# Where 11 modulation sums are worked off, and two later steps for a pair of transposes

## The chip, the cores and the metric

The kernel runs on one core of one Trainium2 chip. The metric is the device time of one launch in microseconds (us): 2756.03 us is the median of three runs before the change (2755.0 to 2768.02). One more execution was profiled; its rows are quoted below.

## What is computed

Two transformer blocks over 256 tokens of width 2048, all in fp32. The part that matters here is the first block, and a piece of the second.

```python
mod = silu(c) @ w_ada + b_ada              # c: one row of 2048, w_ada: 2048 x 12288
sh1, sc1, gt1, sh2, sc2, gt2 = split(mod, 6)
h = modulate(rms_norm(x, g_mix), sh1, sc1)
z = h @ w_in                               # heads q, k, v of two kinds, an indexer, two gates
o_sb = stick_breaking_attention(...)       # 8 heads
o_ds = indexer_sparse_attention(...)       # indexer scores, best 64 keys a query, 8 heads
merged = sigmoid(gate_sb) * (o_sb @ w_o_sb) + sigmoid(gate_ds) * (o_ds @ w_o_dsa)
x = x + gt1 * (merged @ w_out)
h = modulate(rms_norm(x, g_ffn), sh2, sc2) # then a gated FFN with sc2, sh2, gt2
```

The second block has its own projections, 8 heads of a sparse attention (compressed, selected and window branches: `nsa_head`), 8 heads of a forgetting attention (`fox_head`), an output projection and an FFN.

## The kernel before

**Weights.** Every fp32 weight tile (128 x 1024, 512 KB, two k-slices of a 512-column group) is loaded by SyncE into one of 6 buffers `raw` (L127), split by ScalarE into a high part `wh` (L296, 4 buffers) and by VectorE into the rest `wl` (L303, 4 buffers), and then multiplied: in a group with `pair` two matmuls a slice and 128-column strip (L344, L345; L341, L342 for the first), otherwise three (L347 to L349). A strip is accumulated in one of four PSUM tiles `pg`; when its last slice is in, its evacuation (ScalarE and VectorE, L452/L453 for gates, L1050 and L1062 for the two merges) frees it for the next group. Weight tiles are split three tiles ahead of their matmuls (`AHEAD`, L368, `split_to`, L389).

**Modulation sums.** The products with `w_ada` don't run on TensorE. `w_ada` is held transposed; a half row block (128 x 1024, again 512 KB in a `raw` buffer) is multiplied by the broadcast row `cb` and summed by one VectorE instruction (L311). Two such sums give 128 values of `mod`; 192 sums are in the kernel. They stand in the same list of items as the weight tiles, and both are loaded, split and summed in the order of that list, so where a sum is put into the list decides whose neighbour it is on SyncE and on VectorE.

**The list.** `add_group` (L985) appends a group's weight tiles, and after each tile it adds `rate` to a credit; when the credit reaches 1 it appends one sum. In the stretch of the change the groups follow each other so (each with 8 weight tiles, the projections' with 4):

- `ggs[0]` to `ggs[3]` (L1033): the first gate's 16 strips, four groups. Beside them run the last heads of the stick-breaking attention, then `bias_table` (L713, which writes a table `tabs` of 1.5 MB to DRAM), the scoring of `indexer` (L738), and its eight rounds of picking keys.
- four groups of `w_o_sb` (L1054), the first projection of heads, which beside the running sums of `indexer` on GpSimd (L795) merge into the gates.
- `ggs[4]` to `ggs[7]` (L1056): the second gate, with the 8 sparse heads of block one.
- four groups of `w_o_dsa` (L1086), the second projection of heads; each strip is merged by VectorE (L1062) and GpSimd (L1063) and split for the next product by ScalarE (L477) and GpSimd (L479).
- what is left: `while ada_rest and ada_rest[0][2]` (L1087) appends the rest of a begun block of eight sums, the others go to `ada_late` (L1089), which four groups of `w_out` take up at 0.75 a tile, from the fifth tile on.

A program walk through this list gives, for the sums after each group's tiles: 4, 6, 7, 7 in `ggs[0]` to `ggs[3]`; 7 in `w_o_sb`; 8, 7, 7, 7 in `ggs[4]` to `ggs[7]`; 7 in `w_o_dsa`, 1 left, and 16 in `w_out`.

**Steps.** The attention parts are Python generators. `spent` (L323) advances all of them by one step for every 1.27 us of nominal matmul time (`TICK`), so that their instructions stand at fixed places between the matmuls. `yield from wait(3)` passes three steps. `seq` (L690) starts one `nsa_head` every 7 steps. A head computes two score tiles, two softmax tiles (`t`, tag `t2`, two buffers), scales them by rows, passes `W` = 3 steps (L1538), transposes both (L1539, L1540, six matmuls of L846), copies them and multiplies by the values. `fox_chain` (L1636) begins when the last `nsa_head` is done, one head every 5 steps; the second half of the output projection first drains it (L1696): the rest of its steps is issued with no weight matmuls between.

Of the kernel before, what the change touches and what calls it, by code (L numbers as in the profile page):

```python
# [26 lines left out]
W = 3  # L27
# [6 lines left out]
RL = (0.75, 0.6)  # L34
MORE = 12
SPARE = 5
RA = (0.6, 0.7, 0.9, 0.9, 0.45)
GAPS = (5, 7)

LAND = 45  # L40
# [81 lines left out]
def kernel(ctx: ExitStack, tc: tile.TileContext, t):  # L122
# [97 lines left out]
    def wait(n):  # L220
        for _ in range(n):
            yield

    def drain(gens):
        while any(g in active for g in gens):
            tick()
# [13 lines left out]
    def w_items(g):  # L240
        return [("w", [g], k, n) for k, n in pieces(g.nk, g.width)]
# [200 lines left out]
    def copy(out_, in_, scale=None):  # L442
        if alt():
            nc.scalar.activation(out=out_, in_=in_, func=AF.Copy, scale=1.0 if scale is None else scale)
        elif scale is None:
            nc.vector.tensor_copy(out=out_, in_=in_)
        else:
            nc.vector.tensor_scalar(out=out_, in0=in_, scalar1=float(scale), scalar2=None, op0=OP.mult)
# [217 lines left out]
    def av_out(a, vs, o_pair, h, extra=None):  # L666

        O = psm()
        if not isinstance(a, list):
            a = [a]  # L670
        for half in range(2):
            o = O[:, 128 * half:128 * half + 128]
            mms = []
            if extra is not None:
                mms.append((extra[0], extra[1][:, 128 * half:128 * half + 128]))
            for p, (v, c) in zip(a, vs):
                if half == 0:
                    mms.append((v[:, 0, c:c + 128], p[:, 0:128]))
                else:
                    mms.append((v[:, 0, c:c + 128], p[:, 128:256]))  # L680
                    mms.append((v[:, 1, c:c + 128], p[:, 256:384]))
            for n, (l, r) in enumerate(mms):
                nc.tensor.matmul(o, l, r, start=(n == 0), stop=(n == len(mms) - 1))  # L683
        yield
        hi, lo = o_pair(h)
        nc.scalar.activation(out=hi, in_=O[:, :T], func=AF.Copy)
        yield
        nc.vector.tensor_sub(out=lo, in0=O[:, :T], in1=hi.bitcast(F32))
# [123 lines left out]
    def scores(q, k):  # L812

        S = psm()
        nc.tensor.matmul(S[:, 0:128], q[:, 0:128], k[:, 0:128], start=True, stop=True)
        nc.tensor.matmul(S[:, 128:384], q[:, 128:256], k, start=True, stop=True)  # L816
        return S

    def softmax(S, add, pool, shift=None):

        p = pool.tile([128, 384], F32, name="t2", tag="t2")
        st = pool.tile([128, 6], F32, name="st", tag="st", bufs=4)
        for b, (o, n) in enumerate(BLK):
            nc.vector.tensor_tensor_reduce(out=p[:, o:o + n], in0=S[:, o:o + n], in1=add[:, o:o + n], scale=1.0,  # L824
                                           scalar=-3.4e38, op0=OP.add, op1=OP.max, accum_out=st[:, b:b + 1])
        if shift is None:
            nc.vector.tensor_scalar(out=st[:, 2:4], in0=st[:, 0:2], scalar1=-1.0, scalar2=None, op0=OP.mult)
        else:
            nc.vector.tensor_add(out=st[:, 0:2], in0=st[:, 0:2], in1=shift)
            nc.vector.tensor_sub(out=st[:, 2:4], in0=shift, in1=st[:, 0:2])  # L830
        yield
        for b, (o, n) in enumerate(BLK):
            lut(out=p[:, o:o + n], in_=p[:, o:o + n], func=AF.Exp, bias=st[:, 2 + b:3 + b],
                accum_out=st[:, 4 + b:5 + b])
        yield
        return p, st

    def scale_rows(p, r):
        for b, (o, n) in enumerate(BLK):
            nc.vector.tensor_scalar(out=p[:, o:o + n], in0=p[:, o:o + n], scalar1=r[:, b:b + 1], scalar2=None,  # L840
                                    op0=OP.mult)

    def transpose_p(p):
        PT = psm()
        for j in range(3):
            nc.tensor.transpose(PT[:, 128 * j:128 * j + 128], p[:, 128 * j:128 * j + 128], C["ident"])  # L846
        return PT
# [131 lines left out]
    ada_rest = extra + ada_at((2, 3, 8, 9, 10, 11, 4, 5, 6))  # L979
# [5 lines left out]
    def add_group(g, fill=None, rate=0.0, skip=0):  # L985
        for n, it in enumerate(w_items(g)):
            items.append(it)
            if n < skip:
                continue
            credit[0] += rate * it[3] * it[1][0].width / RAW if fill else 0.0  # L990
            while fill and credit[0] >= 1.0:
                items.append(fill.pop(0))
                credit[0] -= 1.0
# [36 lines left out]
    for u, g in enumerate(ggs[:4]):  # L1030
        if u == 1:
            g.pre = lambda: drain([gens["sb"]])
        add_group(g, ada_rest, RA[min(u, 2)])  # L1033

    def o_act(which):
        def act(k):
            return (*bufs["o_" + which](k), bufs["o_" + which].both(k))
        return act

    def sig(which, u):  # L1040
        def go():
            if u % 2 == 0:
                g = gates[which, u // 2]
                lut(out=g, in_=g, func=AF.Sigmoid)
        return go

    def merge1(u):
        def evac(f, ps):
            g = gates[0, u // 2][:, 4 * (u % 2) + f, :]
            nc.vector.tensor_mul(out=g, in0=ps[:, :T], in1=g)  # L1050
        return evac

    for u in range(4):
        add_group(Group("f", [(512, t["w_o_sb"], 512 * u, idr)], 8, o_act("sb"), merge1(u), pre=sig(0, u)), ada_rest, RA[4])  # L1054
    for g in ggs[4:]:
        add_group(g, ada_rest, RA[3])  # L1056

    def merge2(u):
        def evac(f, ps):
            k = 4 * u + f  # L1060
            g = gates[1, u // 2][:, 4 * (u % 2) + f, :]
            nc.vector.tensor_mul(out=g, in0=ps[:, :T], in1=g)  # L1062
            nc.gpsimd.tensor_tensor(out=g, in0=g, in1=gates[0, u // 2][:, 4 * (u % 2) + f, :], op=OP.add)  # L1063
            if k == 0:
                acts["m"] = Pair()
            pend(hilo_gen(*acts["m"](k), g))
        return evac
# [16 lines left out]
    for u in range(4):  # L1084
        add_group(Group("f", [(512, t["w_o_dsa"], 512 * u, idr)], 8, o_act("ds"), merge2(u),
                        pre=dsa_pre if u == 0 else sig(1, u)), ada_rest, RA[4])  # L1086
    while ada_rest and ada_rest[0][2]:  # L1087
# [436 lines left out]
    def nsa_head(h):  # L1524
        g, qh = h // 4, R["qn"][:, h, :]
        sd = R["t"].tile([128, 384], F32, name="t1", tag="t1")
        nc.scalar.activation(out=sd, in_=C["dist"], func=AF.Copy, scale=2.0 ** -(h + 1))
        yield
        S1 = scores(qh, R["kv"][:, 4 + g, :])
        yield  # L1530
        S2 = scores(qh, R["kv"][:, 6 + g, :])
        p1, st1 = yield from softmax(S1, sd, R["t"])
        p2, st2 = yield from softmax(S2, sd, R["t"])
        for i, (p, st) in enumerate(((p1, st1), (p2, st2))):
            nc.vector.reciprocal(out=st[:, 0:2], in_=st[:, 4:6])
            nc.vector.tensor_mul(out=st[:, 0:2], in0=st[:, 0:2], in1=R["gat"][:, 1 + i, h, :])
            scale_rows(p, st[:, 0:2])
        yield from wait(W)  # L1538
        PT1 = transpose_p(p1)  # L1539
        PT2 = transpose_p(p2)  # L1540
        yield
        pT = []
        for PT in (PT1, PT2):
            x = R["t"].tile([128, 384], F32, name="t3", tag="t3", bufs=3)
            copy(x, PT[:, :384])
            pT.append(x)
        yield from wait(W)
        j = h // 2
        vc = R["vcT"][32 * j:32 * j + 32, 128 * (h % 2):128 * (h % 2) + 128]
        yield from av_out(pT, [(R["vsw"], 128 * g), (R["vsw"], 256 + 128 * g)], oN(), h,  # L1550
                          extra=(vc, R["pcT"][32 * j:32 * j + 32, :]))
# [3 lines left out]
    def nsa_chain():  # L1555
        waits = gens["kn"] + gens["qn0"] + gens["qn1"] + [gens["cmp"]]
        while any(g in active for g in waits):
            yield
        yield from cmp_branch()
        yield  # L1560
        yield from seq([nsa_head(h) for h in range(8)], 7)
# [191 lines left out]
```

## Time and profile before

| | us |
|---|---|
| median of three runs | 2756.03 |
| the profiled execution, its time | 2759.37 |
| its span (first to last instruction) | 2757.6 |
| TensorE busy | 2666.0 (97%) |
| VectorE busy | 1982.8 (72%) |
| ScalarE, GpSimd busy | 1364.7, 542.1 |
| granted TensorE clock over the span | 0.991 |

The busy share is an average over stages. The rows below cut the stretch of the change at the first matmul of each group.

### The profile page before, as it was taken

To read this page: it belongs to the slowest core of one execution; us is meant where nothing else is said; L and a number is where in the kernel's file an instruction comes from. 1 tells how busy PE (TensorE), PEld (TensorE's weight loads), DVE (VectorE), ACT (ScalarE), POOL (GpSimd) and SP (SyncE) were. 2 spreads that over 40 slices of the span, in tenths; PEclk is the share of its full clock that TensorE was granted. 3 is DMA by queue.
4 is the path that set the end of the run, shared out by engine and by line. 5 is a ranking of instruction groups with operands and counts; after the bars stand their busy time and mean duration, and the time that the engine had idled before them with its cause. 6 is when DMAs were issued, how large, how long until landed. Compare 5 with 4: busy or idle time off the path is not lost. (4 is left out here: it accounts for less than half of the span.)

```text
span 2757.6 us, 42269 instructions
## 1 busy us (share of the span) xinstructions
PE 2666.0 (97%) x15956; PEld 2336.8 (85%) x15956; DVE 1982.8 (72%) x2882; ACT 1364.7 (49%) x2067; POOL 542.1 (20%) x506
## 2 busy tenths in 40 slices
PE   6899999899998999999999999999999999999999
PEld 5788897798977888888888878888888888888888
DVE  7998986998887876556666756677876665566655
ACT  4554563354446555434555535555555544345443
POOL 1654420210612010000011301102222210012210
PEclk8999999999998999999999999999999999999999
DMA  8888867889986876666666675544566666666664
GB/s 324 264 267 262 260 215 201 277 278 334 311 276 202 299 251 186 194 188 189 189 183 198 188 221 154 161 125 150 175 184 185 195 192 192 191 190 189 189 199 143
DMA packets 302044, 591.16 MB, mean 214 GB/s; under 512 B 20996, under 2 KB 60780, under 8 KB 301710
## 3 DMA queue, kind: packets, MB, share of 16 engines
q1 hardware_dynamic: 298214, 583.61, 66.1%
q10 hardware_dynamic: 3626, 4.85, 0.8%
q8 instruction: 125, 2.05, 0.3%
q14 instruction: 79, 0.65, 0.1%
HBM read 582.54 MB, written 5.78 MB: 213 GB/s over the span
## 5 line engine op out<-in xcount | busy, mean ns | idle before, releaser
L345 PE MATMUL pg<-ring,wh 128*128 128x512 f32 x5408 | 1903.5, 393 | 3.8 <-DVE ring L1165 3.8
L303 DVE TENSOR_TENSOR wl<-raw,wh 128x1024 fp32r<-128x1024 f32 (+1 forms) x921 | 1150.2, 1261 | 623.8 <-ACT wh L296 618.5
L344 PE MATMUL pg<-ring,wl 128*128 128x256 f32 x5408 | 1523.6, 282 | 6.7 <-DVE wl L303 6.2
L296 ACT ACTIVATE wh<-raw 128x1024 fp32r<-128x1024 f32 (+2 forms) x922 | 931.5, 1026 | 879.8 <-PE pg L345 653.9
L345 PEld LDWEIGHTS pg<-ring,wh 128*128 128x128 f32 x5408 | 1019.2, 188 | 217.2 <-DVE ring L1165 5.4
L344 PEld LDWEIGHTS pg<-ring,wl 128*128 128x128 f32 x5408 | 1018.1, 188 | 36.5 <-issue 10.3
L479 POOL TENSOR_TENSOR ring<-gy,ring 128x256 fp32r<-128x256 f32 x88 | 109.9, 1259 | 749.9 <-ACT ring L477 749.9
L347 PE MATMUL pg<-ring,wh 128*128 128x256 f32 x652 | 185.6, 285 | 23.7 <-ACT ring L599 14.0
L349 PE MATMUL pg<-ring,wl 128*128 128x256 f32 x652 | 183.7, 282 | 7.3 <-DVE wl L303 7.1
L348 PE MATMUL pg<-ring,wh 128*128 128x256 f32 x652 | 184.3, 283 | 0.0
L341 PE MATMUL pg<-ring,wh 128*128 128x512 f32 x352 | 144.3, 410 | 10.8 <-DVE ring L1165 4.9
L347 PEld LDWEIGHTS pg<-ring,wh 128*128 128x128 f32 x652 | 123.6, 190 | 27.1 <-ACT ring L599 14.5
L464 POOL TENSOR_TENSOR ring<-pt,ring 128x256 f32<-128x256 f32 x95 | 110.3, 1166 | 142.3 <-ACT pt L463 142.0
L311 DVE CUSTOM_DVE_ANT_0 raw<-raw,cb,mod 128x1024 f32<-128x1024 f32 x96 | 134.8, 1404 | 0.5 <-DVE wl L303 0.3
L311 DVE CUSTOM_DVE_ANT_0 raw<-raw,cb,vec 128x1024 f32<-128x1024 f32 x96 | 130.7, 1361 | 1.9 <-DMA cb<-cdram 1.5
L349 PEld LDWEIGHTS pg<-ring,wl 128*128 128x128 f32 x652 | 123.4, 189 | 9.7 <-DVE wl L303 9.7
L348 PEld LDWEIGHTS pg<-ring,wh 128*128 128x128 f32 x652 | 123.3, 189 | 0.8 <-DVE ring L603 0.2
L1228 POOL TENSOR_TENSOR gy<-ga,rb 128x256 f32<-128x256 f32 x44 | 52.5, 1203 | 325.2 <-ACT ga L203 325.2
L342 PE MATMUL pg<-ring,wl 128*128 128x256 f32 x352 | 99.6, 283 | 0.0
L360 PE MATMUL pg<-wh,ring 128*128 128x512 f32 (+3 forms) x236 | 83.4, 354 | 0.0
L341 PEld LDWEIGHTS pg<-ring,wh 128*128 128x128 f32 x352 | 66.9, 190 | 17.6 <-issue 9.9
L362 PE MATMUL pg<-wh,ring 128*128 128x512 f32 (+3 forms) x236 | 79.0, 335 | 0.0
(294 smaller groups left out, 2485.1 us busy)
## 6 DMA issues: line engine op xcount, KB each, us to landing
raw<-in_w_in SPq DMA_DIRECT2D x240, 512.0 KB, 4.8
raw<-in_w_adaT SPq DMA_DIRECT2D x192, 512.0 KB, 5.2
raw<-in_w_gate SPq DMA_DIRECT2D x176, 512.0 KB, 4.5
raw<-in_w_up SPq DMA_DIRECT2D x176, 512.0 KB, 4.4
raw<-in_w_down SPq DMA_DIRECT2D x176, 512.0 KB, 4.3
raw<-in_w_out SPq DMA_DIRECT2D x64, 512.0 KB, 5.4
raw<-in_w_o_sb SPq DMA_DIRECT2D x16, 512.0 KB, 5.6
raw<-in_w_o_dsa SPq DMA_DIRECT2D x16, 512.0 KB, 6.0
```

Of the source, the lines that this page charges most:

```text
L296: nc.scalar.activation(out=hi, in_=src, func=AF.Copy)
L303: nc.vector.tensor_sub(out=lo, in0=src, in1=hi.bitcast(F32))
L311: nc.vector.tensor_tensor_reduce(out=r, in0=r, in1=P["cb"][:, RAW * half:RAW * half + RAW], scale=1.0, scalar=below, op0=OP.mult, op1=OP.a ...
L341: nc.tensor.matmul(g.ps[f], hi[:, fs], both, start=True, stop=False)
L342: nc.tensor.matmul(ps, lo[:, fs], xh, start=False, stop=False)
L344: nc.tensor.matmul(ps, lo[:, fs], xh, start=False, stop=False)
L345: nc.tensor.matmul(g.ps[f], hi[:, fs], both, start=False, stop=stop)
L347: nc.tensor.matmul(ps, hi[:, fs], xh, start=start, stop=False)
L348: nc.tensor.matmul(ps, hi[:, fs], xl, start=False, stop=False)
L349: nc.tensor.matmul(ps, lo[:, fs], xh, start=False, stop=stop)
L464: nc.gpsimd.tensor_tensor(out=y, in0=x, in1=y, op=OP.add)
L479: nc.gpsimd.tensor_tensor(out=lo, in0=src, in1=hi.bitcast(F32), op=OP.subtract)
```

## The change

```diff
-RA = (0.6, 0.7, 0.9, 0.9, 0.45)
+RA = (0.5, 0.15, 0.3, 0.9, 0.7, 1.0)
...
-        add_group(g, ada_rest, RA[min(u, 2)])
+        add_group(g, ada_rest, RA[u])
...
     for u in range(4):
         add_group(Group("f", [(512, t["w_o_sb"], 512 * u, idr)], 8, o_act("sb"), merge1(u), pre=sig(0, u)), ada_rest, RA[4])
     for g in ggs[4:]:
-        add_group(g, ada_rest, RA[3])
+        add_group(g, ada_rest, RA[5])
...
-        yield from wait(W)
+        yield from wait(W + 2)
         PT1 = transpose_p(p1)
         PT2 = transpose_p(p2)
```

The rates of sums a tile become 0.5, 0.15, 0.3 and 0.9 in `ggs[0]` to `ggs[3]` (they were 0.6, 0.7, 0.9, 0.9), 0.7 in both projections of heads (0.45) and 1.0 in `ggs[4]` to `ggs[7]` (0.9). The transposes of `nsa_head`, and all that follows in a head, come two steps later.

The same walk through the list gives after the change: 4, 1, 2, 7 in `ggs[0]` to `ggs[3]`; 11 in `w_o_sb`; 8 in each of `ggs[4]` to `ggs[7]`; 12 in `w_o_dsa`, then 7 left that L1087 appends (8 sums in a row between the last tile of `w_o_dsa` and the first of `w_out`), and 8 in `w_out`.

## Rows read from the trace of the kernel before

**Rows 1.** The page: busy time and share of each engine.
```profile
PE 2666.0 (97%) x15956; PEld 2336.8 (85%) x15956; DVE 1982.8 (72%) x2882; ACT 1364.7 (49%) x2067; POOL 542.1 (20%) x506
```

**Rows 2.** Windows by group: length, PE PEld DVE ACT POOL, clock, DMA share, GB/s.
```profile
469.22:504.40 35.18, 28.34 (x140) 22.34 (x141) 30.10 (x66) 13.51 (x21) 0.31 (x1) 0.95 0.79 248
504.40:530.53 26.13, 24.02 (x128) 20.82 (x128) 25.82 (x54) 10.04 (x13) 0.21 (x1) 0.93 0.90 309
530.53:583.51 52.98, 50.34 (x417) 49.57 (x418) 47.36 (x80) 28.48 (x37) 23.38 (x17) 1.00 0.79 257
...
660.22:682.41 22.19, 22.19 (x130) 19.54 (x128) 19.40 (x26) 9.59 (x12) 0.00 (x0) 1.00 0.93 336
682.41:728.06 45.65, 45.65 (x385) 45.65 (x384) 39.84 (x46) 25.26 (x32) 30.78 (x25) 1.00 0.93 311
...
750.93:775.50 24.57, 23.43 (x129) 19.49 (x129) 21.29 (x29) 9.62 (x13) 3.16 (x3) 1.00 0.90 305
775.50:800.03 24.53, 23.19 (x129) 19.58 (x129) 21.45 (x29) 9.96 (x13) 3.83 (x4) 1.00 0.87 292
800.03:834.50 34.47, 24.07 (x131) 19.93 (x130) 24.93 (x39) 15.97 (x23) 6.62 (x7) 0.88 0.68 222
```

**Rows 3.** Waits of PE from 469 to 584: total, times, longest.
```profile
PE pg L344 <- DVE wl L303: 4.1, 3, 2.8
PE pg L341 <- DVE ring L453: 3.3, 2, 2.8
PE pg L347 <- DVE ring L1050: 2.6, 2, 1.5
PE pg L347 <- DVE ring L453: 2.1, 1, 2.1
```

**Rows 4.** Timeline of ACT at 466: start, length, what, idle before.
```profile
465.86 1.06 ACT L296 ACTIVATE wh<-raw 128x1024 fp32r<-128x1024 f32 x1 [8.82 <-DMA raw<-in_w_in]
```

**Rows 5.** Instructions on tile tabs: ns shortest/median/longest, first and last start.
```profile
L723 ACTq DMA_DIRECT2D tabs<-t x1: 816/816/816, 443.4 to 443.4; - x1
```

**Rows 6.** Timeline of SP: issues of loads before and beside that write.
```profile
440.27 0.34 SPq L266 DMA_DIRECT2D raw<-in_w_adaT  x1
...
459.83 7.11 SPq L273 DMA_DIRECT2D raw<-in_w_in  x2
```

**Rows 7.** DVE groups, 640 to 682: count, busy us, mean ns, idle before.
```profile
L311 DVE CUSTOM_DVE_ANT_0 raw<-raw,cb,mod 128x1024 f32<-128x1024 f32 x6 | 7.7, 1281 | 0.0
```

**Rows 8.** Groups of DVE and POOL, 696 to 728, beside w_o_dsa.
```profile
L311 DVE CUSTOM_DVE_ANT_0 raw<-raw,cb,mod 128x1024 f32<-128x1024 f32 x3 | 5.3, 1758 | 0.0
...
L479 POOL TENSOR_TENSOR ring<-ring 128x256 fp32r<-128x256 f32 x11 | 18.7, 1719 | 0.0
```

**Rows 9.** Timeline of DVE at the end of w_o_dsa.
```profile
722.20 1.75 DVE L311 CUSTOM_DVE_ANT_0 raw<-raw,cb,mod 128x1024 f32<-128x1024 f32 x1
...
724.31 3.01 DVE L303 TENSOR_TENSOR wl<-raw,wh 128x1024 fp32r<-128x1024 f32 x2 [0.35 <-ACT wh L296]
```

**Rows 10.** Timeline of PE: the first matmul of w_out.
```profile
728.06 0.39 PE L341 MATMUL pg<-ring,wh 128*128 128x512 f32 x1
```

**Rows 11.** Timeline of PE at the first sparse head of block two.
```profile
1777.23 0.70 PE L846 MATMUL pm<-con,t 128*128 128x128 f32 x3 [2.12 <-DVE t L840]
```

**Rows 12.** Windows of all eight sparse heads and of that stall.
```profile
1756.00:1888.00 132.00, 129.73 (x751) 109.71 (x750) 92.94 (x229) 73.22 (x153) 11.88 (x8) 0.99 0.44 128
1768.00:1783.00 15.00, 12.73 (x62) 9.95 (x61) 10.60 (x24) 9.20 (x19) 2.53 (x2) 0.89 0.45 135
```

**Rows 13.** Waits, 1756 to 1888: softmax for the transposes before it.
```profile
DVE t L824 <- PE pm L846: 1.4, 3, 0.7
```

**Rows 14.** Timeline of PE where the forgetting heads are drained.
```profile
1973.60 0.70 PE L846 MATMUL pm<-con,t 128*128 128x128 f32 x3
1975.08 0.94 PE L683 MATMUL pm<-t,ringv 128*128 128x128 f32 x6 [0.78 <-ACT t L444]
1975.77 0.48 PE L341 MATMUL pg<-ring,wh 128*128 128x512 f32 x1
```

## The prediction

> **What bounds the kernel now.** The page comes first: TensorE is busy for 97% of the span [rows 1], so only its stops and its slow clock can be won back, and they have to be looked for stage by stage. Next come the windows cut at the groups. The column PE is to be read against the length: the last group of the second gate, 22.19 us with nothing beside it and no stop, is what eight weight tiles cost at full clock, and the two groups beside the picking of keys take 35.2 and 26.1 us, with VectorE busy for 30.1 and 25.8 of them [rows 2]. The waits then name the releaser: 9.5 us of TensorE's stops in these two groups and 2.6 us beside `w_o_sb` end with a VectorE instruction [rows 3]. The granted clock is 0.95 and 0.93 there, a mean of the two levels 2.4 and 1.2 GHz, and 1.00 where TensorE doesn't stop: 0.05 x 35.2 + 0.07 x 26.1 = 3.6 us of full-speed work are lost as well [rows 2]. Last, why VectorE is late: at 466 ScalarE had waited 8.8 us for a weight tile [rows 4]. The table `tabs` is being written from 443 on [rows 5], and an issue of SyncE that took 0.34 us before it takes 7.11 us for two beside it [rows 6]. So the loads are thin just there, and each sum in the list takes one of six buffers from a weight tile. When the tiles come, VectorE has tiles, scores, key picking and 14 sums to do at once.
>
> **The change part by part.** Nothing is computed more or less: 192 sums stay. I work from the profiled execution, 2759.37 us (span 2757.6); it lies 3.3 us above the median of 2756.03, so I give differences and take them from the median.
>
> *A. Sums leave the selection of keys.* `ggs[1]` and `ggs[2]` lose 5 sums each (6 to 1, 7 to 2). For TensorE that is at most 9.5 + 2.6 + 3.6 = 15.7 us [rows 2, 3]. Six buffers now hold five to six weight tiles, not three, when the table is written, so I take the starvation at 466 as gone. VectorE in `ggs[2]` falls from 30.1 by 5 x 1.28 [rows 7] to 23.7 us. In `ggs[3]` its 25.8 us stay, against 22.2 of matmuls: 3.6 short. In `w_o_sb` four sums come in: 47.4 + 4 x 1.28 to 1.76 [rows 7, 8] = 52.5 to 54.4 us, against 50.3 busy on TensorE: 2.2 to 4.1 short. The cover is the lead of three tiles, 3 x 22.19 / 8 = 8.3 us, just enough for both; the evacuation waits of 2.6 us stay, and I leave 0.6 for what doesn't fit. A = -12.5 us, between -15.7 and 0 (no gain, if the write of the table alone starves the tiles).
>
> *B. Sums go beside `w_o_dsa`.* This stage has TensorE at 45.65 of 45.65 us and VectorE at 39.8 [rows 2]. It gets 11 more sums: 12 in place of 7 among the tiles and 7 in place of 1 after them, and what counts is that eight in a row then stand between the last tile of `w_o_dsa` and the first of `w_out`. In VectorE's queue the first splits of `w_out` and, behind them, the evacuations that free the PSUM tiles wait behind them. Before, a single sum stood there, the first `w_out` split was done at about 725.8 (half of a pair that began at 724.31), and its matmul started at 728.06: a lead of 2.3 us [rows 9, 10]. A sum costs 1.28 us with GpSimd silent [rows 7] and 1.76 beside its merges [rows 8]. The 11 cost 14.1 to 19.4 us; I take 17.5, four at 1.76 and seven between the two at 1.5, because the merges end during the row. Idle VectorE time covers 45.65 - 39.84 = 5.8, the lead 2.3: TensorE starts `w_out` 9.4 us later, between 6.0 and 14.4 (the idle time then reached only in part, 2.7 us). A stop of that length should cost clock: stops of 2.8 us went with 1.8 us lost a group, and the stage from 800 to 834, with 10.4 us of stops, lost 0.12 x 34.5 = 4.1 [rows 2, 3]. I take 1.7, between 0 and 4.1. The other way, `w_out` has 8 sums for 16: its groups of 24.57 and 24.53 us stand 4.7 us over 22.19 [rows 2]; I take back 3.5, between 1 and 4.7. B = +9.4 + 1.7 - 3.5 = +7.6, between +1.3 and +17.5.
>
> At this place a rule of the Trainium skill speaks against the change. [Rows 8] show a sum beside GpSimd at 1.76 for 1.28 us, 0.48 more. The page "SBUF — State Buffer", section "Who interferes with whom", says that a VectorE instruction with two SBUF inputs and a GpSimd instruction that reads SBUF exclude each other for a whole instruction. Taken for every pair it would make each sum wait out a GpSimd instruction; the row bears out a part of that, and the full price is the second rival below.
>
> *C. One more sum in each of `ggs[5]` to `ggs[7]`.* VectorE has room there (19.4 of 22.2 us), DMA hardly (336 GB/s at a share of 0.93) [rows 2]. Three tiles of 0.524 MB are 4.7 us of loads at that rate. I take +1, between 0 and +4.7. The first group keeps its 4 sums, its rate of 0.5 changes nothing.
>
> *D. Transposes two steps later.* The first sparse head stops TensorE for 2.12 us because its row scaling is late [rows 11], and the clock there is 0.89 over 15 us, 1.7 us lost [rows 12]. The scaling was done at about 1777.2, and eight heads of 16 steps, seven apart, make 65 steps in 132 us, some 2 us a step (an estimate), so two steps cover it: -3.8, between -3.8 and 0. Two costs stand against it. The next head's first softmax writes a `t2` buffer that the transposes read; its wait on them is 1.4 us in three cases today [rows 13], and as it is issued at the step where they used to stand, it now waits two steps, 4 us, in seven heads: 28 us, where VectorE idles 132.0 - 92.9 = 39.1 [rows 12]. Behind it in the queue are weight splits (three tiles ahead, covered) and evacuations at a group's end (not covered). I take +2, between 0 and +28. And `fox_chain` starts when the last sparse head ends, so two steps more are left for the drain, where no matmul covers them: today it takes 1973.60 to 1975.77, 0.78 of it idle [rows 14]. What moves in is an exponential and a row scaling; I take +2, between 0 and +4. D = +0.2.
>
> *Sum.* -12.5 + 7.6 + 1.0 + 0.2 = -3.7 us: 2755.7 for a profiled execution, 2752.3 as a median; I write 2752.
>
> **The rivals.**
> *The row of sums finds room (faster).* `w_o_dsa` idles 5.8 us on VectorE, and in the second and third `w_out` group VectorE is busy for 87% only [rows 2]. Had the row been worked off early, B would be about 0: -12.5 + 0 + 1 + 0.2 = -11.3, 2745. Against it: a split pair ends at 727.3, a little before its matmuls [rows 9, 10].
> *The row of sums blocks the second projection (slower).* Each of the 11 waits out a GpSimd instruction: 1.28 + 1.72 = 3.0 us [rows 7, 8], 33 in all, less 5.8 and 2.3: 24.9. B = +24.9 + 1.7 - 3.5 = +23.1, the total +11.8, 2768. Place: VectorE's queue ahead of the first `w_out` split. It decides for slower than before when B is over 11.3, that is from (11.3 + 1.8 + 8.1) / 11 = 1.9 us a sum. Against it: 1.76 [rows 8]. This is the result by the rule of the Trainium skill named above.
> *The softmax waits reach TensorE (slower).* If five of the seven waits of 4 us fall on evacuations, D is -3.8 + 2 + 20 = +18.2, the total +14.3, 2770. For it: the wait exists [rows 13]. Against it: 39 us of idle time [rows 12].
> *The selection doesn't win (the change doesn't do what it says).* The table's write slows the loads whatever stands in the list; A is -4, the total +4.8, 2761. For it: SyncE's issue of 7.11 us [rows 6]; against it: ten buffers fewer go to sums there.
>
> **How the numbers follow.** Chances: forecast 0.50, room 0.17, block 0.13, softmax 0.08, no win 0.12. The forecast's own range is 2744 to 2760 (A to -15 or -8, B from +2 to +12, D -4 to +5). The range for 8 in 10 is 2739 to 2765: below, the first rival with all of A; above, no win and part of the block; left out are the two slow rivals' upper parts. 0.5% of 2756, which is what can be told from no change, is 13.8 us, so faster means below 2742.2 and slower above 2769.8. Faster: 40% of the first rival and a tenth of the forecast, 0.12. Slower: a third of the block and half of the softmax case, 0.08. Same: 0.80.
>
> **What would show it.** Right: `ggs[2]` at 26 to 28 us and `ggs[3]` at 24 to 26, with clock 1.00; ScalarE's wait for a tile at 466 below 3 us; eight sums in a row before the first `w_out` split and TensorE stopped there for 6 to 12 us on `wl`; the second and third `w_out` groups below 23.5 us; no stop at the first sparse head, VectorE waiting on L846 for 15 to 28 us, a drain some 2 us longer. Wrong: `ggs[2]` still over 32 us (A), a stop before `w_out` under 3 or over 16 us (B), TensorE stopped for over 5 us in the sparse heads (D).

## The result and the profile after

The changed kernel takes 2776.96 us (median of five; 2775.15 to 2789.08), the kernel before 2756.03 in the same series. The ratio on record is 1.0055, 95% interval 1.0029 to 1.0082 (it is not the quotient of the two medians, which is 1.0076): slower, where 2752 was forecast, and above the range. The times of most kernels here lie in two bunches some 12 us apart (the last section says what differs), so I compare stretches of the profiled executions, cut at the first matmul of a group as in [rows 2], and use times second.

The span went from 2757.6 to 2775.7 us. TensorE is busy for 4 us more; the rest, 14 us, is time in which it stands.

```profile
PE 2670.3 (96%) x15956; PEld 2341.1 (84%) x15956; DVE 1980.9 (71%) x2882; ACT 1365.1 (49%) x2067; POOL 544.4 (20%) x506
```

Windows of the changed kernel by group (length, PE PEld DVE ACT POOL, clock, DMA share, GB/s): `ggs[2]`, `ggs[3]`, `w_o_sb`, the last gate group, `w_o_dsa`, the first three of `w_out`. They answer to [rows 2].

```profile
468.61:494.13 25.52, 25.52 (x141) 21.19 (x141) 23.47 (x54) 10.79 (x15) 0.31 (x1) 1.00 0.82 250
494.13:519.32 25.19, 22.44 (x130) 19.40 (x128) 24.92 (x50) 11.18 (x15) 0.22 (x1) 0.99 0.86 293
519.32:576.55 57.23, 53.74 (x417) 53.25 (x418) 53.99 (x88) 28.68 (x37) 27.51 (x18) 0.92 0.82 270
654.25:677.46 23.21, 22.71 (x129) 19.40 (x127) 19.98 (x27) 9.63 (x13) 0.00 (x0) 1.00 0.98 354
677.46:739.88 62.42, 45.55 (x384) 44.46 (x385) 53.07 (x69) 25.53 (x32) 27.93 (x25) 0.95 0.94 323
739.88:764.40 24.52, 24.52 (x129) 21.13 (x129) 18.50 (x24) 11.01 (x15) 9.32 (x9) 0.92 0.94 332
764.40:786.99 22.59, 22.59 (x129) 19.50 (x128) 19.57 (x25) 9.23 (x12) 3.22 (x3) 1.00 0.82 278
786.99:809.58 22.59, 22.59 (x129) 19.51 (x128) 13.79 (x18) 10.30 (x14) 5.66 (x6) 1.00 0.65 213
```

The reader is to see that `ggs[2]` has become stop-free (PE equals the length, 35.2 to 25.5 us), that `w_o_sb` has lost 4.25 (clock 0.92, VectorE at 54 of 57), and that `w_o_dsa` is 16.8 us longer with no more matmul work in it.

ScalarE near 466, against the 8.82 us wait for a tile in [rows 4]: its splits and evacuations there now wait about 1 us at a time, for TensorE.

```profile
458.05 1.06 ACT L298 ACTIVATE wh<-raw 128x1024 fp32r<-128x1024 f32 x1 [1.06 <-PE pg L347]
...
468.15 2.00 ACT L298 ACTIVATE wh<-raw 128x1024 fp32r<-128x1024 f32 x2
```

TensorE's waits in the changed kernel (total, times, longest), in `ggs[2]` to `w_o_sb`, then in `w_o_dsa`; lines are two higher than before:

```profile
PE pg L349 <- DVE ring L1052: 3.5, 2, 2.0
PE pg L349 <- DVE ring L455: 2.8, 1, 2.8
...
PE pg L343 <- DVE ring L1064: 9.9, 1, 9.9
PE pg L349 <- DVE ring L1064: 4.3, 3, 1.9
PE pg L351 <- DVE wl L305: 2.7, 2, 1.4
```

The stop of 9.9 us lies behind the row of sums. VectorE's timeline there, which answers to [rows 9]:

```profile
726.61 1.29 DVE L313 CUSTOM_DVE_ANT_0 raw<-raw,cb,mod 128x1024 f32<-128x1024 f32 x1
...
734.22 1.28 DVE L313 CUSTOM_DVE_ANT_0 raw<-raw,cb,mod 128x1024 f32<-128x1024 f32 x1
...
736.92 2.48 DVE L305 TENSOR_TENSOR wl<-raw,wh 128x1024 fp32r<-128x1024 f32 x2 [1.41 <-ACT wh L298]
739.32 1.41 DVE L1064 TENSOR_TENSOR ring<-pg,ring 128x256 f32<-128x256 f32 x4
```

After the last sum VectorE waits for ScalarE, splits a pair of `w_out`, and only then runs L1064, the evacuations that free `w_o_dsa`'s last PSUM tiles. TensorE waited for those up to 739.88. The kernel before has the same order in its queue, right behind the last line of [rows 9], where nothing waited for it:

```profile
727.24 1.44 DVE L1062 TENSOR_TENSOR ring<-pg,ring 128x256 f32<-128x256 f32 x4
```

At the sparse heads, VectorE's wait on the transposes and TensorE's waits from 1763 to 2010; they answer to [rows 13] and [rows 11]:

```profile
DVE t L826 <- PE pm L848: 25.6, 6, 6.1
```

```profile
PE pm L848 <- DVE st L826: 5.4, 7, 1.0
PE pg L343 <- DVE ring L1135: 3.1, 2, 2.6
PE pm L848 <- DVE t L842: 2.5, 1, 2.5
```

The drain, in TensorE's timeline (against [rows 14], where 0.78 us of it was idle, now 3.5):

```profile
1987.85 0.91 PE L685 MATMUL pm<-t,ringv 128*128 128x128 f32 x6 [0.47 <-DVE t L448]
1991.21 0.70 PE L848 MATMUL pm<-con,t 128*128 128x128 f32 x3 [2.46 <-DVE t L842]
1992.49 1.00 PE L685 MATMUL pm<-t,ringv 128*128 128x128 f32 x6 [0.58 <-ACT t L446]
```

The drain is part of a stretch of seven groups behind the sparse heads. Its window in the kernel before and in the changed one, with the columns of [rows 2]:

```profile
1926.87:2021.01 94.14, 89.61 (x522) 77.07 (x521) 80.92 (x158) 50.78 (x91) 24.86 (x25) 1.00 0.55 172
```

```profile
1938.18:2039.21 101.03, 93.78 (x531) 80.58 (x530) 84.17 (x166) 52.04 (x95) 27.01 (x26) 0.97 0.54 167
```

Over the whole stretch TensorE stands for 7.3 us, 4.5 before, its clock has fallen to 0.97, and nine more matmuls are in it; beside the sparse heads there are ten fewer.

### The profile page after: what moved, and what is told of

The parts are those of the page before. It is cut to its first block, busy times and chain, and to the rows that moved or that the text cites. A ratio compares the mean times of both kernels' runs of the same rounds, so it can differ in the third digit from the quotient of the medians.

```text
span 2775.7 us, 42268 instructions
## 1 busy us (share of the span) xinstructions
PE 2670.3 (96%) x15956; PEld 2341.1 (84%) x15956; DVE 1980.9 (71%) x2882; ACT 1365.1 (49%) x2067; POOL 544.4 (20%) x506
## 4 chain that ended last, share of the span: by engine, by line
PE 77%; DVE 13%; issue 4%; DMA 3%; ACT 2%; POOL 1%; ACTq 0%; SPq 0%; DVEq 0%; POOLq 0%
PE pg L347 41%; PE pg L346 21%; DVE wl L305 5%; DVE raw L313 4%; PE pg L343 3%; PE pg L344 1%; DMA raw<-in_w_in 1%; PE pm L685 1%; ACT wh L298 1%; PE pg L362 1%; PE pg L351 1%; PE pg L364 1%; PE pg L363 1%; PE pg L350 1%; PE pg L349 1%
## 5 line engine op out<-in xcount | busy, mean ns | idle before, releaser
L346 PEld LDWEIGHTS pg<-ring,wl 128*128 128x128 f32 x5408 | 1017.9, 188 | 29.6 <-issue 10.3
L351 PE MATMUL pg<-ring,wl 128*128 128x256 f32 x652 | 186.2, 286 | 9.9 <-DVE wl L305 9.8
L351 PEld LDWEIGHTS pg<-ring,wl 128*128 128x128 f32 x652 | 126.1, 193 | 12.8 <-DVE wl L305 12.8
L343 PEld LDWEIGHTS pg<-ring,wh 128*128 128x128 f32 x352 | 67.7, 192 | 23.1 <-issue 20.0
L362 PE MATMUL pg<-wh,ring 128*128 128x512 f32 (+3 forms) x236 | 83.5, 354 | 0.0
L344 PEld LDWEIGHTS pg<-ring,wl 128*128 128x128 f32 x352 | 67.9, 193 | 13.9 <-issue 0.2
```

Source lines behind the costliest of these rows:

```text
L343: nc.tensor.matmul(g.ps[f], hi[:, fs], both, start=True, stop=False)
L344: nc.tensor.matmul(ps, lo[:, fs], xh, start=False, stop=False)
L346: nc.tensor.matmul(ps, lo[:, fs], xh, start=False, stop=False)
L351: nc.tensor.matmul(ps, lo[:, fs], xh, start=False, stop=stop)
L362: nc.tensor.matmul(ps, xh[:, bs], hi, start=start, stop=False)
```

## The experiments

The stretches in one table (us, from the profiled executions, cut as above). `FFN` is the stretch from 911 to 1603 of the kernel before, `heads` the five groups beside the sparse heads (1762 to 1927), `drain` the seven behind them (to 2021); 834 to 911 and 1603 to 1762 are left out, and `e6` and `e8` stand in the text.

| | before | after | e1 | e2 | e3 | e4 | e5 | e7 | e9 | e10 |
|---|---|---|---|---|---|---|---|---|---|---|
| `ggs[1]` to `[3]` | 98.7 | 87.5 | 87.6 | 99.0 | 87.5 | 87.5 | 87.6 | 87.6 | 87.6 | 87.6 |
| `w_o_sb` | 53.0 | 57.2 | 55.9 | 52.7 | 57.6 | 57.5 | 55.9 | 53.9 | 53.9 | 53.9 |
| `ggs[4]` to `[7]` | 98.9 | 100.9 | 102.0 | 99.6 | 100.6 | 101.7 | 101.2 | 101.7 | 102.1 | 100.0 |
| `w_o_dsa` | 45.7 | 62.4 | 62.0 | 45.7 | 51.7 | 56.2 | 61.3 | 49.7 | 48.5 | 45.7 |
| `w_out` | 106.4 | 104.0 | 104.0 | 104.9 | 102.8 | 104.4 | 103.3 | 105.2 | 104.5 | 107.6 |
| FFN, 911 to 1603 | 692.1 | 692.7 | 703.6 | 705.3 | 705.4 | 693.0 | 693.9 | 703.6 | 691.6 | 693.7 |
| heads | 165.0 | 166.5 | 165.6 | 166.6 | 164.0 | 164.0 | 159.8 | 165.6 | 162.2 | 162.2 |
| drain | 94.1 | 101.0 | 94.5 | 101.2 | 92.5 | 94.3 | 102.9 | 94.4 | 94.0 | 92.9 |

Each column is one execution, and the same schedule does not always take the same time: `w_o_sb` with the change's rate took 55.9 to 57.6 us in seven executions, the heads with the old wait 164.0 to 165.6 in five, and the stretch from `ggs[1]` to 911, the same in `e7` and `e9`, 476.2 and 472.3. A difference of one or two us in a row is no result by itself.

**The transposes alone, and the sums alone.** Theory: each part costs where it stands. Rival: what the heads lost follows from the sums.

`e1_old_wait`, after with

```diff
-        yield from wait(W + 2)
+        yield from wait(W)
```

> The changed kernel with the sparse heads' transposes back at their old step (the sums stay where the change put them). Theory, each part costs at its own place: the stage of the sparse heads gives back its +8.3 us (stretch 1757 to 1985 of the changed kernel against the kernel before), so about 2777 - 8 = 2769; VectorE's waits on the transposes fall from 25.6 us in six to about 5 in three, and the first sparse head's stop of 2.1 us is back. Rival, the loss there follows from the sums (everything arrives some 10 us later and loads fall otherwise): 2777 within 3, and the groups of that stage stay as long as in the changed kernel.

Median 2775.56 of 12, ratio to before 1.0042 (1.0021 to 1.0063). Heads and drain together 260.1 us, 267.6 in the changed kernel, 259.2 before; VectorE's wait on the transposes is 1.4 us in three again. The median by itself would suit the rival (2777 within 3); but the profiled execution took 11 us longer in the FFN, which the edit doesn't touch (last section), and the stretch that it does touch gave back 7.5 us.

`e2_only_wait`, before with the opposite edit.

> The kernel before with the sparse heads' transposes two steps later and nothing else. Theory, each part costs at its own place: 2756 + 8 = 2764, first stop of the heads gone, VectorE waits on the transposes 25 us in six, TensorE's transposes wait about 0.7 us a head on VectorE. Rival, the loss follows from the sums: 2756 within 3. By the prediction's own step D (+0.2): 2756.

Median 2771.32 of 12, ratio 1.0034 (1.0012 to 1.0056); the time lies above both expectations, and here too the FFN took 13 us longer. Heads and drain 267.8 us, and the wait is the one of the changed kernel:

```profile
DVE t L824 <- PE pm L846: 26.0, 6, 6.1
```

The groups of the heads move by the same amounts as in the changed kernel (-3.6, +2.7, +4.1 for the first three, -1.6 for the last two together). The theory holds: the later transposes cost 7.5 us with the sums (`e1`) and 8.6 without (`e2`). The rival falls.

**Softmax wait or drain.** `e5_third_buffer`, after with

```diff
-        p = pool.tile([128, 384], F32, name="t2", tag="t2")
+        p = pool.tile([128, 384], F32, name="t2", tag="t2", bufs=3 if pool is R.get("t") else None)
...
-        pc = R["c"].tile([128, T], F32, name="pcT")
+        pc = ef
```

The second cut makes room for the buffer.

> The changed kernel with a third buffer for the softmax tile of the sparse heads (room made by writing the transposed compressed probabilities into the tile they came from). Theory, softmax wait: the next head's first softmax no longer waits for the transposes two steps on, VectorE's waits on them fall from 25.6 us to under 6, the groups in that stage lose 2.7 + 4.1 + 3.7 of excess while the first head's gain of 3.6 stays: about 2777 - 9 = 2768. Rival, the drain: the heads' end is still two steps later, and what costs is the work left without cover, 2.8 + 1.4 us: at least 2774.

Median 2771.34 of 10, ratio 1.0032 (1.001 to 1.0055). VectorE's waits in the heads, then TensorE's:

```profile
DVE t L826 <- PE pm L818: 3.6, 3, 1.9
...
DVE t L826 <- PE pm L848: 1.6, 2, 1.1
```

```profile
PE pg L343 <- DVE ring L1135: 2.7, 2, 2.2
PE pm L848 <- DVE t L842: 2.5, 1, 2.5
```

The wait on the transposes is nearly gone, and the heads go from 166.5 to 159.8 us, 5.2 under before. The drain stays 8.8 us over before, with the same two stops. So both theories hold, each for its own stretch: 6.7 us for the wait, 6.9 (in the changed kernel) for the drain. The 6.9 are not all new time: some matmuls have moved into that stretch, and the last two groups of the heads, where they stood, are 1.6 us shorter.

`e6_end_in_place`, after with the wait behind the transposes shortened, so that a head ends where it did:

```diff
-        yield from wait(W)
+        yield from wait(W - 2)
         j = h // 2
```

> The changed kernel with two steps taken out behind the transposes (the wait ahead of the products with the values is W - 2), so that a sparse head ends at the step where it ended before. Theory, softmax wait: the transposes are as late as in the changed kernel, so VectorE still waits 25 us on them; only the drain's part of 2.8 + 1.4 us goes, and the products with the values may now wait for the copies: 2773 to 2778. Rival, the drain: the forgetting heads start two steps earlier and all but the first cost goes: about 2769.

Median 2789.33 of 4, ratio 1.0098 (1.0059 to 1.0136): outside both expectations. TensorE now waits ahead of the products with the values for the copies of the transposed rows:

```profile
PE pm L685 <- DVE t L448: 13.5, 7, 3.3
```

The heads took 188.6 us, but the drain 93.2, that of before. The test of the softmax wait was spoilt by the new stop; for the drain it suggests that its price hangs on the step at which the last head ends.

`e8_first_head_only`, after with

```diff
-        yield from wait(W + 2)
+        yield from wait(W if h else W + 2)
```

> The changed kernel, but only the first of the eight sparse heads has its transposes two steps later. Theory: the first head's stop of 2.1 us and its low clock stay away (-3.6), one softmax waits instead of six (+1), the last head ends where it did before, so the drain costs nothing: the stretch from 1757 to the end of the drain is 2 to 4 us shorter than with the old step everywhere, 260 us there, so about 257. Rival, the heads are tied by their spacing: moving one moves its neighbours' waits, 260 to 263.

Median 2774.62 of 10, ratio 1.0031 (1.001 to 1.0053). Heads and drain 257.5 us, in the expected range, yet not for the reason given: the first head's stop fell from 2.1 to 1.0 us and the second head, now five steps behind it, stops TensorE as well,

```profile
PE pm L817 <- DVE st L826: 1.9, 1, 1.9
```

so the heads took 164.3 us, and `e3`, with the old wait everywhere, 164.0 (256.5 with the drain). What differs from `e1`'s 165.6 is the clock at the first stop (last section). The edit gained nothing that shows; by its mechanism, though not by its 260 to 263, the rival is the nearer one.

**Row or density beside `w_o_dsa`.** The two are taken apart with the old wait in the heads. `e3_no_row`: 12 sums among the tiles, the row's seven sent to `w_out`.

```diff
-    while ada_rest and ada_rest[0][2]:
-        items.append(ada_rest.pop(0))
     ada_late[:0] = ada_rest
```

> Sums as the change spreads them among the tiles (12 beside w_o_dsa), transposes at their old step, but the seven sums that the change puts in a row behind w_o_dsa go to w_out (15 there in place of 8). Theory, the row is the stop: the stretch from w_o_dsa's first matmul to w_out's, 45.7 us before and 62.0 with the row, comes to 47 to 50 (five sums more among its tiles than before, at about 1.5 us each, against 5.8 us of idle time), w_out's second and third group go back from 22.6 to about 24.5: some 10 us under the run with the row. Rival, density: it is the 12 sums among the tiles that starve w_o_dsa, as its waits on sums inside the stage say (4.3 and 2.7 us): at least 56 us.

Ratio 1.0005 (0.9987 to 1.0023). Windows and TensorE's waits of `w_o_dsa` and the second `w_out` group:

```profile
675.86:727.55 51.69, 47.39 (x385) 46.67 (x385) 44.52 (x56) 25.73 (x32) 28.40 (x25) 0.97 0.93 319
...
750.15:772.74 22.59, 22.59 (x129) 19.51 (x128) 21.15 (x29) 9.71 (x13) 4.30 (x4) 1.00 0.96 348
```

```profile
PE pg L349 <- DVE ring L1064: 2.9, 3, 1.9
PE pg L351 <- DVE wl L305: 1.4, 1, 1.4
```

`e4_row_at_old_rate`: eight sums among the tiles, and the row of seven.

```diff
-RA = (0.5, 0.15, 0.3, 0.9, 0.7, 1.0)
+RA = (0.5, 0.15, 0.3, 0.9, 0.7, 1.0, 0.45)
...
-                        pre=dsa_pre if u == 0 else sig(1, u)), ada_rest, RA[4])
-    while ada_rest and ada_rest[0][2]:
+                        pre=dsa_pre if u == 0 else sig(1, u)), ada_rest, RA[6])
+    while len(ada_rest) > 4:
```

> The other corner: eight sums among the tiles of w_o_dsa (rate 0.45 as before) and the row of seven kept, 12 sums in w_out, transposes at their old step. Theory, the row is the stop: the stretch of w_o_dsa is 45.65 plus the stop in front of w_out of about 8 to 10 us, so 54 to 56, clock falling in the stop. Rival, density: 47 to 50, since VectorE comes to the row early enough.

Ratio 1.001 (0.9988 to 1.0033). Window of `w_o_dsa` and its largest wait:

```profile
677.76:733.99 56.23, 46.17 (x384) 45.78 (x385) 48.23 (x61) 25.35 (x32) 28.00 (x25) 0.94 0.92 321
```

```profile
PE pg L343 <- DVE ring L1064: 9.6, 1, 9.6
```

The two add up. Density alone costs 51.7 - 45.7 = 6.0 us (`e3`), the row alone 56.2 - 45.7 = 10.6 (`e4`); that makes 16.6, and `e1`, which has both, took 16.3 more than the kernel before. (By `e1` against `e3` the row costs 10.3.) The row theory is right for the larger part, and its expectation for density (47 to 50) was too low. I had not expected `w_out`: with 15 sums its second and third group took 22.6 and 23.1 us, with eight 22.6, where the kernel before, with 16, took 24.6 and 24.5.

**A version that keeps the gain.** `e7_spread`, with the old wait, no row (as `e3`), and a rate of its own for `w_o_dsa` (as `e4`, the last of the list):

```diff
-RA = (0.5, 0.15, 0.3, 0.9, 0.7, 1.0)
+RA = (0.6, 0.3, 0.3, 0.9, 0.55, 1.0, 0.5)
```

> A version meant to keep what the change won: rates 0.6, 0.3, 0.3, 0.9 in the first four gate groups, 0.55 in w_o_sb, 1.0 in the last four gate groups, 0.5 in w_o_dsa, no row, 19 sums in w_out, transposes at their old step. Theory, each part at its own place: ggs[2] stays at 25.5 to 26.5, w_o_sb at 53 to 55, the last gate groups +2, w_o_dsa 45.7 to 47, w_out +3 for three sums more: -11 + 1 + 2 + 1 + 3 = -4 against the kernel before. Rival, the loads set the pace wherever the sums stand (0.524 MB each): what ggs[2] gains comes back in w_out and w_o_dsa, 0 within 2 against before.

Ratio 0.9983 (0.9959 to 1.0007), which can't be told from no change. From `ggs[1]` to the FFN at 911, the table's rows and the 78 us that follow: 476.2 us against 479.4 before, -3.2, near the theory's -4 but within what one execution can tell (`e9`, with the same schedule, has 472.3). And `w_o_dsa` took 49.7 us with eight sums, for which it had 45.7 before, so part of the rival seems to hold: L351 waits 2.9 us on splits there, behind gate groups with eight sums each.

`e9_five_heads`, the same with the third buffer of `e5` and

```diff
-        yield from wait(W)
+        yield from wait(W + 2 if h < 5 else W)
```

> The spread of the run before with 19 sums in w_out, and with it a third softmax buffer and the transposes two steps later in the first five sparse heads only, so that the last head ends where it did before. Theory, softmax wait and drain are two separate costs: the four groups of the sparse heads take 160 us as with the third buffer (165 before), the drain 94 as before (103 with the third buffer and all eight heads late): 254 to 256 for the stretch, so about 5 us under the run with the spread alone. Rival, the sixth head, now five steps behind the fifth, stops TensorE as the second head did when only the first was late (2.1 us), and the drain stays longer: 258 to 261.

Ratio 0.998 (0.996 to 0.9999). Heads 162.2, drain 94.0, 256.2 in all, against 260.0 in `e7`: the two costs come apart, and the gain is 3.8, not 5, since the last two groups of the five (46.0 us, 43.9 in `e5`) are back at the time of before. Against the heads that had the old wait without a fall of the clock at the first stop (`e3`, `e4`: 164.0) the gain is 1.8. The stop at the sixth head that the rival named did not come.

`e10_five_heads_fewer_late`, the same with

```diff
-RL = (0.75, 0.6)
+RL = (0.8, 0.6)
...
-RA = (0.6, 0.3, 0.3, 0.9, 0.55, 1.0, 0.5)
+RA = (0.6, 0.3, 0.3, 0.9, 0.5, 0.95, 0.5)
```

> The same with rates 0.5 in w_o_sb, 0.95 in the last gate groups and 0.8 in w_out (22 sums there). Theory, sums set the pace in w_o_sb and the gate groups: w_o_sb 52.7 to 53.5 (53.9 in the spread run), the last gate groups 1 us less in all, w_out 1 us more: 0 to 2 us under the run beside it. Rival, loads set the pace from 583 on: what the gate groups lose comes back in w_out, 0 within 1.

Median 2755.37 of 12, before 2759.93, ratio 0.9967 (0.9946 to 0.9987): a little faster than the kernel before, as `e9` is. A walk through the list gives 21 sums in `w_out`, one fewer than expected. Windows of `w_o_sb`, `w_o_dsa` and the last of `w_out`:

```profile
520.97:574.82 53.85, 51.69 (x418) 50.79 (x418) 47.75 (x82) 29.08 (x37) 23.36 (x17) 0.97 0.81 261
674.83:720.49 45.66, 45.66 (x386) 45.65 (x385) 40.42 (x48) 25.48 (x32) 31.70 (x25) 1.00 0.94 327
...
790.71:828.11 37.40, 24.39 (x131) 19.91 (x130) 31.48 (x50) 16.20 (x23) 6.14 (x7) 0.87 0.79 274
```

Two us fewer in the gate groups and three in `w_o_dsa` than `e9`, three more in `w_out`, two more in the FFN's first groups: from `ggs[1]` to 911 both take 472.3 us. Within that stretch the loads or sums only change place, as the rival said; no run takes the two apart.

## Why the prediction was wrong

The sum was -3.7 us for the profiled execution, and +18.1 came. Of the error of 21.8 us, D has 8.2, B 6.7, A 5.5 and C 1.0.

*A, forecast -12.5, measured -7.0.* The selection of keys went much as forecast: -11.2 in `ggs[1]` to `ggs[3]`, clock 1.00, ScalarE's wait of 8.8 us gone (from 431 to 520 it still waits for tiles, 11.5 us in five, but TensorE waits for no split there). The failed step is "the lead of three tiles ... just enough for both". I had found VectorE 2.2 to 4.1 us short in `w_o_sb` and let the lead cover it; it came out 4.25 longer (2.9 to 4.6 in the seven executions at this rate). On a split TensorE waited nowhere there, so the lead did cover those; it doesn't cover the evacuations, and TensorE waits for them (L455 at the end of `ggs[3]` 2.8 us, L1052 3.5, where L1050 had 2.6 before). The larger part is the clock, which the working left out of this stage: 0.92 in place of 1.00, and TensorE busy for 53.7 in place of 50.3 us with the same matmuls. At a rate of 0.5 to 0.55 the stage takes 53.9 (`e7`, `e10`).

*B, forecast +7.6, measured +14.3.* The start of `w_out` was forecast 9.4 us late and came 16.8. Two subtractions of the working fell. The 5.8 us of idle VectorE time in `w_o_dsa` were not to be had: five sums more among the tiles cost 6.0 by themselves (`e3`), in evacuations and splits that came late and a clock of 0.97. And the lead of 2.3 us on the first `w_out` split was beside the point, as the split is not what ends last: the stop ends with L1064, the evacuations of `w_o_dsa`'s own PSUM tiles. I had named them as waiting behind the row, and then counted the split's lead alone. So nothing covers the row: the seven sums that it adds are 9.0 us at 1.28, and they cost 10.3 to 10.6; the wait of 1.41 us for ScalarE behind the last sum is about what is left. Clock: 1.7 forecast, 0.08 x 24.5 = 2.0 in `w_out`'s first group. `w_out` as a whole is 2.4 us shorter with that loss in it; its second and third group gave back 3.9, where I took 3.5. It is not for the fewer sums: `e3` had 15 there and all but the same groups. Each time `w_o_dsa` was longer; that its loads ran ahead meanwhile is my reading, and wasn't tried apart.

The rival in which each sum waits out a GpSimd instruction named the place, not the price: beside merges a sum took 1.75 us, in the row 1.28 to 1.29, never 3.0. Its price came of a misread row: the 1.72 us of a GpSimd instruction in [rows 8] hold GpSimd's own wait for VectorE. In the kernel before the same instruction took 0.74 us where VectorE stood idle:

```profile
695.24 0.74 POOL L479 TENSOR_TENSOR ring<-ring 128x256 fp32r<-128x256 f32 x1
...
706.45 1.72 POOL L479 TENSOR_TENSOR ring<-ring 128x256 fp32r<-128x256 f32 x1
```

So both engines are slowed: a sum by 0.47 us, less than a GpSimd instruction alone, and GpSimd by 0.98, less than a sum alone. Waiting out a whole one, a sum would take 1.28 + 0.74 = 2.0 us, an estimate from these rows. The Trainium skill, page "SBUF — State Buffer", section "Who interferes with whom", has a VectorE instruction with two SBUF inputs contend with a GpSimd instruction that reads SBUF, for a port pair that is an exclusive lock; the trace agrees that the two hold each other up, though by about two thirds (0.47 of 0.74) and three quarters (0.98 of 1.28) of the other's instruction and not by a whole one. The row of sums was slow without it.

The signs named beforehand sort the same way: `ggs[2]` (25.5, just under its 26 to 28), the waits of ScalarE, the eight sums and a stop of 6 to 12 us came about as written, though the stop ended on L1064 and not on the split; the sign against D, over 5 us of stops at the sparse heads, came too.

*C, forecast +1, measured +2.0*, inside its bounds (+1.7 to +3.2 in the nine executions at a rate of 1.0); at 0.95 it is +1.1 (`e10`).

*D, forecast +0.2, measured +8.4.* The first stop shrank to 1.0 us and its group won what was forecast (-3.6 for -3.8). Of the two costs set at 2 us each, the softmax wait was sized rightly as a wait (25.6 us for 28) and wrongly in what reaches TensorE: 6.7 us, which a third buffer gives back. The 39 us of idle time in [rows 12] were an average; each wait stands at one place, where the next head's scores, row scaling and evacuations queue behind it. The drain cost 6.9, above its bound of 4 even when the 1.6 us won ahead of it are taken off: I counted the work that moves in (an exponential and a scaling), not that a group before it stops as well (L1135, 2.6 us) and that the clock falls with the stops, to 0.97 over 101 us. `e10`, with the last heads in place, took 92.9 us at a clock of 1.00.

The likeliest case was thus wrong in three places of one kind: idle time or a lead, averaged over a stage, taken as cover for work that has a fixed place in a queue; and in two of the three, A and D, the clock that falls with the stops was left out. The rival of the softmax waits had the right sign: it put D at 18.2, with 20 us of waits reaching TensorE, of which 6.7 did.

## What to carry to other kernels

In this kernel idle time of VectorE covered added work only where what stood behind it in the queue was not awaited: look for the evacuation that frees PSUM, not only for the next operand. A row of optional work at a stage's boundary cost its full length and a little more, while eight sums spread over the same stage cost between nothing and 4 us. A stop has a second price in TensorE's clock, which may come or not. A step moved later lengthened the life of its buffer and the tail at the end of its chain: give it a buffer, and leave the last members of the chain where they were.

## What the runs showed that was not expected

In these traces TensorE has two steady rhythms at the same granted clock. In the stop-free groups of the FFN a group of eight tiles takes 22.19 us in the kernel before and 22.59 in `e1`, with the clock at 1.00 in both:

```profile
1044.67:1066.86 22.19, 22.19 (x130) 19.53 (x129) 15.58 (x22) 12.83 (x20) 0.90 (x2) 1.00 0.63 191
```

```profile
1056.03:1078.62 22.59, 22.59 (x129) 19.49 (x128) 15.51 (x21) 12.77 (x20) 0.99 (x2) 1.00 0.61 186
```

A rhythm once taken lasts: in `e1` every group from 988 to 1570 is 1.8% longer than before. From 911 to 1603 the profiled executions take either 692 to 694 us or 703 to 706 (the table's row), of whatever kernel, which is the distance of the two bunches of times. Where it changed in this stretch, it did so within the first tile of a group, in `e2` behind a stop of 0.45 us, in `e5` and `e6` without one; what picks it stays open. It is worth knowing when two kernels are compared: `e9` and `e10` took 2746 to 2752 or 2758 to 2765 us, the kernel before in their series 2756 to 2762 or 2765 to 2776, some 10 us more in either bunch, while their medians hang on how many executions fell into which.

The same stop doesn't always cost clock. The first sparse head stops TensorE for 2.12 us in the kernel before and in `e3` alike; [rows 12] have the clock at 0.89 around it, and in `e3` it stayed at full. The stop, and the window of its group:

```profile
1785.19 0.59 PE L848 MATMUL pm<-con,t 128*128 128x128 f32 x2 [2.12 <-DVE t L842]
```

```profile
1769.83:1804.57 34.74, 32.33 (x181) 26.58 (x180) 25.95 (x63) 21.39 (x46) 5.97 (x4) 1.00 0.40 124
```

The group took 34.7 us for 35.8, in `e4` as in `e3`; in `e1` and `e7`, where the clock fell, it took 36.3. So a microsecond or more of what the prediction counted as the stop's price need not come with the stop.
